# Griffin-style encoder block in split fp32: operand refills and weight sums dealt out by K tiles, and three more idle products at the start

## The chip, the core and the metric

One core of a Trainium2 chip runs the whole block in one launch. The metric is the device time of one execution in microseconds (us), the median over runs. Names of the engines in the text: PE is TensorE, DVE is VectorE, ACT is ScalarE, POOL is GpSimd, SP is SyncE, which here only issues transfers.

## The reference

A stream of 1,024 tokens, with 16 learned meta tokens ahead of it, goes through one layer of width 1,024 in float32:

```
u = rms_norm(h) * pre_w
rq, rk, rv, rg, aq, ak, av, ag, gr, ga = split(u @ w_in)
o_r = bidirectional_retention(rotary(rq), rotary(rk), rv)      # 4 heads, chunks of 128
y_r = (group_norm(o_r) * ret_nw * silu(rg)) @ w_rb
o_a = windowed_attention(rotary(aq), rotary(ak), av, sink)     # 8 heads, window +-128
y_a = (o_a * silu(ag)) @ w_ab
mix = sigmoid(gr) * y_r + sigmoid(ga) * y_a
out = h + rms_norm(mix @ w_o) * post_w                         # the meta tokens are dropped
```

The change touches the first projection (the columns of rq and rk of the first head) and the four large products at the end: the gates rg, ag, gr, ga (four times 1,024 columns of `w_in`), `w_rb`, `w_ab` and `w_o`.

## The kernel before

**Split products.** Every float32 product is made of three on PE: each operand is split into a rounded high part h (made by ACT or POOL as a copy to the type fp32r) and a low part, operand minus h (made by DVE, `dve_lo`, L92). `mm3` issues high x high (L76), low x high (L77) and high x low (L78).

**The start.** `idle` products multiply zeros by zeros (L313, 128x384) while the first inputs arrive. Then come eight rounds, one for each K tile of 128 rows of x: ACT makes the high part `xh[k]` (L333), DVE the low part `xl[k]` (L335), and `qk0_mm(k)` (L321) issues 18 products over six outputs. Between the rounds stand small serial computations (the decays of the retention).

**The middle.** Retention (four heads), then attention, with gate projections of z filled in between.

**The end: four phases z, r, a, o.** z computes the gates in 16 units, r multiplies by `w_rb`, a by `w_ab`, o by `w_out`. Each unit is a 2x2 block product in seven products instead of eight, in the order 1, 5, 6, 2, 7, 3, 4 (units go in pairs; the first pair of z has an order of its own). The left operands of a unit are sums of its weight blocks (`prepare`: weights `wrz{u}_{j}`, sums `stz{u}S`, split into `lhz{u}_{p}` by ACT, L976, and `llz{u}_{p}` by DVE, L92); they are prepared six products ahead of their use (`LEAD`). What comes out is added up by DVE in `combine` (`u2z`, `u3z`, `c1z`: L1066) and goes on to `post`. In the phase z some partial results `e{u}{p}` come back from DRAM.

**Right operands.** The seven right operands are four plain blocks and sums of the activation: B11, T1 (product 5), T2 (6), B21 (2), T3 (7), B22 (3) and T4 (4), each of four K tiles in a high and a low part. They lie in the tiles `big` and `T` and are overwritten for the next phase as soon as their last product of the old one is done. `refill(nm, src)` brings in the operands of the phase that follows `nm`; it returns which step is to be issued behind which product, counted from the first product of that next phase (negative numbers lie in `nm`): loads of staged tiles (`stage`), differences on DVE (`minus`, L1155), and `split_b` (a copy on ACT, a difference on DVE, L92). After z and after r the sums are made on the spot from the attention's and the retention's gated outputs in DRAM (for r and a); after a the sums of `w_out`, which lie ready in DRAM, are fetched (`get_pre`) and only the plain blocks are split.

**The output weights' sums.** For the phase o the sums T1, T3, T2 and T4 of `w_out` (`SUMS`) are computed during z: `pre_load(k)` fetches the four blocks of a K tile k, and `pre_split(k, behind)` makes four differences, splits each and stores eight tiles to DRAM (`wT1`, `wT3`, `wT2`, `wT4`, and the stores `preT`, L779 and L781). `run` hangs `pre_load(k)` behind product 12k + 16 and `pre_split(k)` behind product 12k + 22, counted from the first product of z.

**What sets the order.** The program text is an order of wishes: a scheduler with a simulated timeline lays out each engine's instructions from it, by priority and by when an instruction could start, and `issue_after` forces one instruction behind another. SP issues the transfers in one row, each at its turn, so a transfer that has to wait holds up the ones behind it.

Of the kernel before, what the change touches and what calls it, by code (L numbers as in the profile page):

```python
# [7 lines left out]
F32 = mybir.dt.float32  # L8
R = mybir.dt.float32r
AF = mybir.ActivationFunctionType  # L10
ALU = mybir.AluOpType
# [23 lines left out]
def cols(c):  # L35
    return (0, NM) if c == 0 else (NM + P * (c - 1), NM + P * c)
# [3 lines left out]
def block_kernel(ctx: ExitStack, tc: tile.TileContext, x0, xT, x, meta, w_in, w_rb, w_ab, w_out, post_w,  # L40
                 rope, tab, out):
    nc = tc.nc
# [12 lines left out]
    def bank(tag, name):  # L55
# [13 lines left out]
    pre_d = {n: [dram.tile([P, 4, 512], F32, tag=f"pre{n}{s}", name=f"pre{n}{s}") for s in range(2)]  # L69
             for n in ("T1", "T2", "T3", "T4")}  # L70
# [20 lines left out]
    def dve_lo(o, i, hi):  # L91
        return nc.vector.tensor_tensor(o, i, hi.bitcast(F32), ALU.subtract).ins  # L92
# [19 lines left out]
    def halves_w(u):  # L112
        hi, lo = [], []

        def split(t, act):
            h, l = (wp.tile([P, 4, 256], R, tag=f"w{x}", bufs=4, name=f"w{x}{u}_{len(hi)}") for x in "hl")
            if act:
                nc.scalar.copy(h, t)
            else:
                pool_hi(h, t)  # L120
            hi.append(h)
            lo.append(l)
            return dve_lo(l, t, h)

        return split, ((lambda k, a, b: hi[k // 4][:, k % 4, a:b]), (lambda k, a, b: lo[k // 4][:, k % 4, a:b]))
# [140 lines left out]
    with tc.tile_pool(name="setup", bufs=1, reuse_waits="tile") as st:  # L266
# [42 lines left out]

        idle = pj("idle")  # L310
        zeros = xm.rearrange("p k e -> p (k e)")
        for i in range(8):
            nc.tensor.matmul(idle[:, 0:KT * (32 + NM)], zeros[:, 0:P], zeros, start=True, stop=True)  # L313


# [38 lines left out]
        split, wv0 = halves_w(U_V)  # L354
# [5 lines left out]
        for c in range(9):  # L360
            a, b = cols(c)
# [372 lines left out]
    def last_keys():  # L734
# [4 lines left out]
    SUMS = ("T1", (0, 0), (0, 1), (0, 0)), ("T3", (0, 1), (1, 1), (0, 1)), ("T2", (1, 1), (1, 1), (0, 0)), (  # L739
        "T4", (1, 0), (1, 0), (1, 1))  # L740
# [23 lines left out]
    def pre_load(k, src):  # L764

        w[k] = {}
        for i, j in ((0, 0), (0, 1), (1, 1), (1, 0)):
            w[k][i, j] = t = stage(f"w{i}{j}{k}", 1)
            src(t, 4 * i + k, j)

    def pre_split(k, behind):

        x = w.pop(k)
        for n, o, a, b in SUMS:
            with tc.issue_after(behind):
                nc.vector.tensor_tensor(x[o], x[a], x[b], ALU.subtract)
            h, l = (stage(f"w{n}{k}{e_}", s, R) for s, e_ in enumerate("hl"))
            nc.scalar.copy(h, x[o])
            nc.sync.dma_start(pre_d[n][0][:, k], h.bitcast(F32))  # L779
            dve_lo(l, x[o], h)  # L780
            nc.sync.dma_start(pre_d[n][1][:, k], l.bitcast(F32))  # L781

    w, near = {}, []
    gates = [U_G + u for u in range(4)] + [U_AG + u for u in range(4)] + [U_GR + u for u in range(8)]
# [151 lines left out]
    def right(n, s, k):  # L936
        if n == "T4" and k == 3:
            return margins[s], lambda t: t.rearrange("p (a c) -> p a c", a=KT)
        return B[n][s][:, k], lambda t: t
    POST = {2: (0, 0), 7: (1, 1), 3: (0, 1), 4: (1, 0)}  # L940
    final = "o", 3, 4
    sub, mul, add = ALU.subtract, ALU.mult, ALU.add

    def stage(name, j=0, dt=F32):
        return (yp if j else lp).tile([P, 512], dt, tag=f"sg{int(j)}", bufs=8 if j else 7, name=name)
# [4 lines left out]
    def split_b(n, k, src):  # L950
        (h, as_), (l, _) = (right(n, s, k) for s in range(2))
        nc.scalar.copy(h, as_(src))
        dve_lo(l, as_(src), h)

    class Phase:
# [18 lines left out]
        def split(self, u, p, src):  # L974
            h, l = (lp.tile([P, 4, P], R, tag=t, bufs=LEAD, name=f"{t}{self.nm}{u}_{p}") for t in ("lh", "ll"))
            nc.scalar.copy(h, src)  # L976
            dve_lo(l, src, h)
            self.ops[u, p] = h, l
# [149 lines left out]
    def get_pre(n):  # L1128
        for s in range(2):
            m = B[n][s].shape[1]  # L1130
            nc.sync.dma_start(B[n][s].bitcast(F32), pre_d[n][s][:, 0:m])
            if m < 4:
                d, as_ = right(n, s, m)
                nc.sync.dma_start(d.bitcast(F32), as_(pre_d[n][s][:, m]))
# [8 lines left out]
    def refill(nm, src):  # L1143

        x = {}

        def load(i, j):
            def f():
                for k in range(4):
                    x[i, j, k] = t = stage(f"{nm}{i}{j}{k}", j)  # L1150
                    src(t, 4 * i + k, j)
            return f

        def minus(o, a, b):
            nc.vector.tensor_tensor(x[*o], x[*a], x[*b], sub)  # L1155

        def plain(n, i, j):
            def f():
                for k in range(4):
                    split_b(n, k, x[i, j, k])  # L1160
            return f

        def t1():
            for k in range(4):
                minus((0, 0, k), (0, 1, k), (0, 0, k))
                split_b("T1", k, x[0, 0, k])

        def t2():
            for k in range(4):
                minus((0, 0, k), (1, 1, k), (0, 0, k))  # L1170
                split_b("T2", k, x[0, 0, k])

        def t3():
            for k in range(4):
                minus((0, 1, k), (1, 1, k), (0, 1, k))

        def b21():
            for k in range(4):
                split_b("B21", k, x[1, 0, k])
                minus((0, 0, k), (1, 0, k), (0, 0, k))  # L1180

        def got(n):
            return lambda: get_pre(n)

        if nm == "a":
            return {-16: [load(0, 0)], -14: [load(1, 1)], -13: [plain("B11", 0, 0)], -11: [got("T1")],
                    -10: [load(1, 0)], -9: [got("T2")], -7: [plain("B21", 1, 0)], -5: [got("T3")],
                    -3: [plain("B22", 1, 1)], -1: [got("T4")]}
        return {-16: [load(0, 0), load(0, 1)], -14: [load(1, 1)], -13: [plain("B11", 0, 0)], -11: [t1],
                -10: [load(1, 0)], -9: [t2, t3], -7: [b21], -5: [plain("T3", 0, 1)], -3: [plain("B22", 1, 1)],  # L1190
                -1: [plain("T4", 0, 0)]}

    def run(phases):

        jobs = [(ph, u, p) for ph, _ in phases for u, p in ph.seq]
        hooks, i = {}, 0
        for ph, src in phases:
            i += len(ph.seq)
            if src:
                hooks.update({i + j: f for j, f in refill(ph.nm, src).items()})  # L1200

        for u in (0, 1):
            hooks.setdefault(len(jobs) - len(ph_o.seq) - 11 + u, []).insert(0, lambda u=u: ph_o.block(u, "A11"))
        for k in range(4):
            hooks[12 * k + 16] = [lambda k=k: pre_load(k, act_src(w_out))]
            hooks[12 * k + 22] = [lambda k=k: pre_split(k, near[0])]
        n = 0
        for i, (ph, u, p) in enumerate(jobs):
            while n < min(i + LEAD, len(jobs)):
                q, u_, p_ = jobs[n]  # L1210
                q.prepare(u_, p_)
                n += 1
            yield
            ph.product(u, p)
            for f in hooks.get(i, ()):
                f()
# [6 lines left out]
    def act_src(d):  # L1223
        def src(o, k, j):
            nc.sync.dma_start(o, d[k, :, 512 * j:512 * j + 512])
        return src
# [122 lines left out]
    def o_tail(o, a):  # L1349
# [4 lines left out]
        if a:  # L1354
            with tc.issue_after(scaled):
                for c, t, _ in parts:
# [6 lines left out]
            (3, 4)]  # L1363
    ph_o = Phase("o", seq, o_load, o_post, apart=(0, 1))
    steps = run([(Phase("z", sequence(16, (1, 3, 2, 5, 6, 7, 4)), w_loader(w_in, gates), z_post, z_fetch,
                        early=(0, 1), pre=PRE),
                  act_src(oTr_d)),
# [211 lines left out]
    i = attention()  # L1579
# [105 lines left out]
```

## Time and profile before

| what | us |
|---|---|
| median of three runs (1043.12, 1043.39, 1044.73) | 1043.39 |
| the profiled execution | 1044.06 |
| its span, first to last instruction | 1042.3 |
| PE busy | 1025.3 (98%) |
| PE's weight loads busy | 898.8 (86%) |
| DVE busy | 834.9 (80%) |
| ACT busy | 502.5 (48%) |
| POOL busy | 227.9 (22%) |

The mean clock that PE was granted is 0.998 of full speed. The page gives the busy time of each engine; the list of waits says for a line how long its engine stood idle ahead of it, and which instruction of another engine ended that (us in total, times, longest); the timeline lists instructions in order with their start, length, engine, line and operation, `out<-in`, and in brackets the idle time before them and what ended it. A row of SPq is a transfer's issue; in the list of transfers the last number is the median time from issue to landing. In a table by stages, the columns behind the busy times of the engines are the granted clock, the busy share of the 16 DMA engines, and the GB/s that they moved. Names of tiles are given without their numbers in the profile's rows: `u2z` stands for the `u2z` tile of any unit.

### The profile page before, as it was taken

The numbers are of one execution on the slowest core, as the hardware profiler recorded it, in microseconds if no ns is written. First come the engines' busy times: TensorE is split into PE (matmuls) and PEld (weight loads), VectorE is DVE, ScalarE is ACT, GpSimd is POOL, SyncE is SP. The second block draws the span as 40 slices with busy tenths as digits, with TensorE's granted clock in tenths as the row PEclk, the third lists the DMA queues.
The fourth block names the chain that finished last, engine by engine and source line by source line (L and its number), as shares of the span: only waits on it lengthen the run. The fifth ranks groups of instructions, "written<-read, shape, count | busy, mean of one in ns | idle before, by whom it ended". The sixth has DMA issues, their size and how long they took to land. (4 is left out here: it accounts for less than half of the span.)

```text
span 1042.3 us, 17315 instructions
## 1 busy us (share of the span) xinstructions
PE 1025.3 (98%) x5880; PEld 898.8 (86%) x5880; DVE 834.9 (80%) x1802; ACT 502.5 (48%) x1129; POOL 227.9 (22%) x368
## 2 busy tenths in 40 slices
PE   8999999999999999999999999999999999999997
PEld 8998999989989888988888888777888788788886
DVE  7786769758876778778769988998899899778665
ACT  5541332523423466664676554555557446334443
POOL 3345244243342433444310000000000000111032
PEclk9999999999999999999999999999999999999999
DMA  9434123243241467675558679899925746789464
GB/s 355 164 84 90 62 45 89 76 79 112 80 93 62 102 174 188 179 194 157 171 174 322 216 255 311 309 317 346 392 106 178 251 156 222 234 219 336 130 122 81
DMA packets 98841, 188.45 MB, mean 181 GB/s; under 512 B 13025, under 2 KB 37633, under 8 KB 98193
## 3 DMA queue, kind: packets, MB, share of 16 engines
q1 hardware_dynamic: 81200, 162.89, 46.4%
q0 software_dynamic: 10176, 14.73, 9.5%
q10 hardware_dynamic: 7376, 9.73, 2.7%
q8 instruction: 46, 0.75, 0.3%
q14 instruction: 43, 0.34, 0.1%
HBM read 124.32 MB, written 57.68 MB: 175 GB/s over the span
## 5 line engine op out<-in xcount | busy, mean ns | idle before, releaser
L1289 POOL DMA_DIRECT2D mx_d<-c1a x4 | 3.6, 890 | 398.1 <-DVE c1a L1280 398.1
L77 PE MATMUL bz<-big,llz 128*128 128x512 f32 x192 | 74.8, 390 | 0.3 <-DVE llz L92 0.3
L76 PE MATMUL bz<-big,lhz 128*128 128x512 f32 x192 | 74.0, 390 | 1.1 <-ACT lhz L976 1.1
L78 PE MATMUL bz<-big,lhz 128*128 128x512 f32 x192 | 74.2, 389 | 0.0
L76 PE MATMUL pv<-wh,big 128*128 128x256 f32 x256 | 72.8, 284 | 0.0
L77 PE MATMUL pv<-wh,big 128*128 128x256 f32 x256 | 72.7, 284 | 0.0
L78 PE MATMUL pv<-wl,big 128*128 128x256 f32 x256 | 72.7, 284 | 0.0
L76 PE MATMUL bz<-T,lhz 128*128 128x512 f32 x176 | 68.2, 390 | 1.4 <-DVE u2z L1066 1.3
L77 PE MATMUL bz<-T,llz 128*128 128x512 f32 x176 | 68.6, 390 | 0.9 <-DVE llz L92 0.9
L78 PE MATMUL bz<-T,lhz 128*128 128x512 f32 x176 | 68.5, 389 | 0.0
L76 PE MATMUL paq<-big,wh 128*128 128x512 f32 x128 | 51.5, 403 | 0.0
L1429 ACT ACTIVATE p<-raw,nm 128x337 f32<-128x337 f32 (+1 forms) x64 | 35.5, 556 | 33.1 <-DVE nm L1426 31.6
L77 PE MATMUL paq<-big,wl 128*128 128x512 f32 x128 | 50.3, 393 | 0.0
L78 PE MATMUL paq<-big,wh 128*128 128x512 f32 x128 | 50.2, 392 | 0.0
L1442 POOL TENSOR_SCALAR p<-p,den 128x336 f32<-128x336 f32 (+2 forms) x60 | 34.6, 624 | 66.7 <-DVE den L1433 64.1
L76 PEld LDWEIGHTS pv<-wh,big 128*128 128x128 f32 x256 | 48.4, 189 | 0.4
L77 PEld LDWEIGHTS pv<-wh,big 128*128 128x128 f32 x256 | 48.3, 189 | 0.4
L78 PEld LDWEIGHTS pv<-wl,big 128*128 128x128 f32 x256 | 48.2, 188 | 0.3
L76 PEld LDWEIGHTS bz<-big,lhz 128*128 128x128 f32 x192 | 36.0, 188 | 8.8 <-ACT lhz L976 1.5
L92 DVE TENSOR_TENSOR wl<-wr,wh 128x1024 fp32r<-128x1024 f32 x28 | 35.1, 1257 | 10.0 <-POOL wh L89 6.8
L77 PEld LDWEIGHTS bz<-big,llz 128*128 128x128 f32 x192 | 36.0, 188 | 8.1 <-DVE llz L92 0.6
L78 PEld LDWEIGHTS bz<-big,lhz 128*128 128x128 f32 x192 | 36.0, 188 | 7.5
(621 smaller groups left out, 3592.8 us busy)
## 6 DMA issues: line engine op xcount, KB each, us to landing
wrz<-in_w_in_dram SPq DMA_DIRECT2D x32, 512.0 KB, 6.1
wr<-in_w_in_dram SPq DMA_DIRECT2D x29, 512.0 KB, 4.1
we<-in_w_in_dram SPq DMA_DIRECT2D x16, 512.0 KB, 4.3
tg<-tg_d SPq DMA_DIRECT2D x32, 256.0 KB, 4.9
e<-e ACTq DMA_DIRECT2D x20, 256.0 KB, 2.6
e<-e SPq DMA_DIRECT2D x20, 256.0 KB, 4.7
xn<-in_x_dram SPq DMA_DIRECT2D x8, 512.0 KB, 9.0
oTr_d<-ost SPq DMA_DIRECT2D x16, 256.0 KB, 2.1
```

Of the source, the lines that this page charges most:

```text
L76: nc.tensor.matmul(o, ah, bh, start=first, stop=False, **kw)
L77: nc.tensor.matmul(o, al, bh, start=False, stop=False, **kw)
L78: latest[:] = [nc.tensor.matmul(o, ah, bl, start=False, stop=last, **kw).ins]
L92: return nc.vector.tensor_tensor(o, i, hi.bitcast(F32), ALU.subtract).ins
L1289: nc.gpsimd.dma_start(d, to, accum_op=ALU.add)
L1429: last["exp"] = nc.scalar.activation(pp[:, x_, w0 - o:w0 - o + 1 + wid], r[:, 0:1 + wid], AF.Exp, scale=-1.0, bias=nm_[:, x_:x_ + 1], accu ...
L1442: nc.gpsimd.tensor_scalar(v, v, den[:, x_:x_ + 1], 1.0, op0=ALU.mult, op1=ALU.mult)
```

## The change

- The start issues 11 idle products instead of 8.
- `pre_split` makes one of the four sums at a call instead of all: they hang behind the products 12k + 21 to 12k + 24, each with its own `near[0]` (DVE's last addition into a unit's result) to be issued behind.
- `refill` deals its steps out by K tiles, one or two to a product instead of four behind one product, After z and r, T2 and B21 come later than before, and T3, B22 and T4 stand behind the products 1 to 8 of the new phase itself; one tile of B21's load is issued eight products later than the others. After a, the splits keep their places but for the dealing out. The operations are the same in number and kind.
- `run` collects several steps for one product in a list.

```diff
--- before.py
+++ after.py
@@ -309,7 +309,7 @@
 
         idle = pj("idle")
         zeros = xm.rearrange("p k e -> p (k e)")
-        for i in range(8):
+        for i in range(11):
             nc.tensor.matmul(idle[:, 0:KT * (32 + NM)], zeros[:, 0:P], zeros, start=True, stop=True)
 
 
@@ -768,17 +768,19 @@
             w[k][i, j] = t = stage(f"w{i}{j}{k}", 1)
             src(t, 4 * i + k, j)
 
-    def pre_split(k, behind):
-
-        x = w.pop(k)
-        for n, o, a, b in SUMS:
-            with tc.issue_after(behind):
-                nc.vector.tensor_tensor(x[o], x[a], x[b], ALU.subtract)
-            h, l = (stage(f"w{n}{k}{e_}", s, R) for s, e_ in enumerate("hl"))
-            nc.scalar.copy(h, x[o])
-            nc.sync.dma_start(pre_d[n][0][:, k], h.bitcast(F32))
-            dve_lo(l, x[o], h)
-            nc.sync.dma_start(pre_d[n][1][:, k], l.bitcast(F32))
+    def pre_split(k, i, behind):
+
+        n, o, a, b = SUMS[i]
+        x = w[k]
+        with tc.issue_after(behind):
+            nc.vector.tensor_tensor(x[o], x[a], x[b], ALU.subtract)
+        h, l = (stage(f"w{n}{k}{e_}", s, R) for s, e_ in enumerate("hl"))
+        nc.scalar.copy(h, x[o])
+        nc.sync.dma_start(pre_d[n][0][:, k], h.bitcast(F32))
+        dve_lo(l, x[o], h)
+        nc.sync.dma_start(pre_d[n][1][:, k], l.bitcast(F32))
+        if n == "T4":
+            del w[k]
 
     w, near = {}, []
     gates = [U_G + u for u in range(4)] + [U_AG + u for u in range(4)] + [U_GR + u for u in range(8)]
@@ -1144,51 +1146,44 @@
 
         x = {}
 
-        def load(i, j):
+        def load(i, j, ks=range(4)):
             def f():
-                for k in range(4):
+                for k in ks:
                     x[i, j, k] = t = stage(f"{nm}{i}{j}{k}", j)
                     src(t, 4 * i + k, j)
             return f
 
         def minus(o, a, b):
-            nc.vector.tensor_tensor(x[*o], x[*a], x[*b], sub)
-
-        def plain(n, i, j):
-            def f():
-                for k in range(4):
-                    split_b(n, k, x[i, j, k])
-            return f
-
-        def t1():
+            return lambda k: nc.vector.tensor_tensor(x[*o, k], x[*a, k], x[*b, k], sub)
+
+        def split(n, i, j):
+            return lambda k: split_b(n, k, x[i, j, k])
+
+        def each(at, n, *fs):
             for k in range(4):
-                minus((0, 0, k), (0, 1, k), (0, 0, k))
-                split_b("T1", k, x[0, 0, k])
-
-        def t2():
-            for k in range(4):
-                minus((0, 0, k), (1, 1, k), (0, 0, k))
-                split_b("T2", k, x[0, 0, k])
-
-        def t3():
-            for k in range(4):
-                minus((0, 1, k), (1, 1, k), (0, 1, k))
-
-        def b21():
-            for k in range(4):
-                split_b("B21", k, x[1, 0, k])
-                minus((0, 0, k), (1, 0, k), (0, 0, k))
+                at.setdefault(n + k if len(fs) > 1 else n + k // 2, []).extend([lambda f=f, k=k: f(k) for f in fs])
 
         def got(n):
             return lambda: get_pre(n)
 
+        at = {-16: [load(0, 0)] + ([] if nm == "a" else [load(0, 1)]), -14: [load(1, 1)]}
+        each(at, -13, split("B11", 0, 0))
         if nm == "a":
-            return {-16: [load(0, 0)], -14: [load(1, 1)], -13: [plain("B11", 0, 0)], -11: [got("T1")],
-                    -10: [load(1, 0)], -9: [got("T2")], -7: [plain("B21", 1, 0)], -5: [got("T3")],
-                    -3: [plain("B22", 1, 1)], -1: [got("T4")]}
-        return {-16: [load(0, 0), load(0, 1)], -14: [load(1, 1)], -13: [plain("B11", 0, 0)], -11: [t1],
-                -10: [load(1, 0)], -9: [t2, t3], -7: [b21], -5: [plain("T3", 0, 1)], -3: [plain("B22", 1, 1)],
-                -1: [plain("T4", 0, 0)]}
+            at.update({-11: [got("T1")], -10: [load(1, 0)], -9: [got("T2")], -5: [got("T3")], -1: [got("T4")]})
+            each(at, -7, split("B21", 1, 0))
+            each(at, -3, split("B22", 1, 1))
+            return at
+        each(at, -11, minus((0, 0), (0, 1), (0, 0)), split("T1", 0, 0))
+        at[-10].append(load(1, 0, range(3)))
+        each(at, -7, minus((0, 0), (1, 1), (0, 0)), split("T2", 0, 0))
+        each(at, -3, split("B21", 1, 0), minus((0, 0), (1, 0), (0, 0)))
+        at[-2].append(load(1, 0, (3,)))
+        at[1] = at.pop(0)
+        each(at, 2, minus((0, 1), (1, 1), (0, 1)))
+        each(at, 3, split("T3", 0, 1))
+        each(at, 5, split("B22", 1, 1))
+        each(at, 7, split("T4", 0, 0))
+        return at
 
     def run(phases):
 
@@ -1197,13 +1192,15 @@
         for ph, src in phases:
             i += len(ph.seq)
             if src:
-                hooks.update({i + j: f for j, f in refill(ph.nm, src).items()})
+                for j, f in refill(ph.nm, src).items():
+                    hooks.setdefault(i + j, []).extend(f)
 
         for u in (0, 1):
             hooks.setdefault(len(jobs) - len(ph_o.seq) - 11 + u, []).insert(0, lambda u=u: ph_o.block(u, "A11"))
         for k in range(4):
             hooks[12 * k + 16] = [lambda k=k: pre_load(k, act_src(w_out))]
-            hooks[12 * k + 22] = [lambda k=k: pre_split(k, near[0])]
+            for i in range(4):
+                hooks[12 * k + 21 + i] = [lambda k=k, i=i: pre_split(k, i, near[0])]
         n = 0
         for i, (ph, u, p) in enumerate(jobs):
             while n < min(i + LEAD, len(jobs)):
```

## The prediction

> **What bounds the kernel now.** I read the page's busy times first, then the list of what TensorE (PE) waited for, then the timeline at the places where it waited.
>
> ```profile
> span 1042.3 us, 17315 instructions
> PE 1025.3 (98%) x5880; PEld 898.8 (86%) x5880; DVE 834.9 (80%) x1802; ACT 502.5 (48%) x1129; POOL 227.9 (22%) x368
> ```
>
> PE is busy for 1025.3 of 1042.3 us, so all of its idle time together is 17.0 us; an edit that leaves the products as they are can win more than that only by the clock, which makes a busy product shorter. The list of PE's waits shows what of it has a releaser on another engine inside the last phases:
>
> ```profile
> PE bz L76 <- DVE u2z L1066: 1.3, 1, 1.3
> PE bz L77 <- DVE llz L92: 1.2, 2, 0.9
> PE bz L76 <- ACT lhz L976: 1.1, 1, 1.1
> PE ba L77 <- DVE lla L92: 0.9, 1, 0.9
> PE br L77 <- DVE llr L92: 0.8, 2, 0.6
> ```
>
> These are bz (phase z), br and ba (the first products after a refill): 5.3 us. The rest lies at the start, where the clock is low. The timeline of the start (start us, length us, engine, line):
>
> ```profile
> 1.36 2.93 PE L313 MATMUL idle<-xm 128*128 128x384 f32 x8 [1.36 <-DVE warm L207]
> 5.53 0.77 PE L76 MATMUL pq<-big,w 128*128 128x512 f32 x1 [1.24 <-ACT big L333]
> 9.77 0.33 PEld L78 LDWEIGHTS pq<-big,w 128*128 128x128 f32 x1
> 10.53 0.19 PEld L76 LDWEIGHTS pq<-big,w 128*128 128x128 f32 x1
> 10.65 0.39 PE L76 MATMUL pq<-big,w 128*128 128x512 f32 x1
> 13.47 0.62 PE L76 MATMUL pq<-big,w 128*128 128x512 f32 x2
> 16.28 0.39 PE L76 MATMUL pq<-big,w 128*128 128x512 f32 x1
> ```
>
> The eight idle products end at 4.29, PE stands for 1.24 us, and the first round of L321 (one k over all six outputs) takes from 5.53 to 10.65, 5.12 us, where a later round takes 16.28 - 13.47 = 2.81 us. A weight load falls from 0.33 to 0.19 us between 9.77 and 10.53: that is where the clock rises, 5.0 us after unbroken work began.
>
> **The change part by part.** The profiled execution took 1044.06 us (span 1042.3 and 1.8 around it), 0.67 above the median 1043.39 of the three timed runs, which lie between 1043.12 and 1044.73. I sum against 1044.06 and give the result as the forecast: the scatter of the runs is about what an earlier or later rise of the clock would make, and the change acts on that very term.
>
> *Eleven idle products.* Three more at 2.93 / 8 = 0.37 us end at 4.29 + 1.10 = 5.39, before the first real product at 5.53, which waits for ACT: they delay nothing, and the gap shrinks from 1.24 to 0.14 us. If what counts is 5.0 us of unbroken work, it now counts from 1.36, and the clock rises at 6.36. Then 0.83 us of the first round run low, 0.83 / 5.12 = 16% of it, and the other 84% take 2.36 us: the round ends at 8.72 instead of 10.65, 1.9 us sooner. Do the inputs keep up?
>
> ```profile
> 7.49 1.16 ACT L333 ACTIVATE big<-xr,vec 128x1040 fp32r<-128x1040 f32 x1 [1.47 <-DVE w L92]
> 8.68 1.30 DVE L335 SCALAR_TENSOR_TENSOR big<-xr,vec,big 128x1040 fp32r<-128x1040 f32 x1 [0.93 <-ACT big L333]
> 9.84 2.44 ACT L333 ACTIVATE big<-xr,vec 128x1040 fp32r<-128x1040 f32 x2 [1.19 <-DMA xr<-in_xT_dram]
> 32.37 0.36 ACT L167 COPY vmeta<-pv 16x256 f32<-16x256 f32 x1 [3.24 <-PE pv L165]
> ```
>
> Round 2's high part is there at 8.65 and its low part at 9.98 (needed for the last third, at about 10.6); round 3's high part at 9.84 + 1.22 = 11.06, needed at 11.53. So 1.9 us is just about what the inputs allow, and no more. The next piece of serial work on ACT waits for PE at 32.37, so it moves up with PE. Bounds: 0 (the clock rises at 10.5 as now) to 2.0.
>
> The Trainium skill, "TensorE: Matmul & The Clock Gate", Part 1, says that the clock is decided at the ends of free-running windows of 4096 cycles, about 3.4 us, and rises after one busy window. By that the present rise at about 10.4 would come one window sooner, near 7.0, and the start would give 1.7 instead of 1.9 us; the trace's single rise cannot tell the two apart.
>
> *The refills dealt out.* Here the diff promises more than it does. I laid the instruction orders of the two built programs side by side: of the refills' differences and splits on DVE (L1155, L92 into big and T), all three phases, every one stands where it stood, but for two pieces of T4 in z's refill that move by one place. From there to the end all engines' orders are the same, with the same waits. The scheduler had already pulled these operations to where their buffers come free. So the stalls around the two refills stay:
>
> ```profile
> 763.38 0.69 DVE L1066 TENSOR_TENSOR u3z<-u3z,bz 128x512 f32<-128x512 f32 x1 [1.39 <-ACT u3z L1063]
> ```
>
> DVE's unbroken run before br starts here, released by a product through ACT, so it starts earlier when PE is earlier and the stall is neither eaten nor added to. Term: 0. It could be 1.7 at most (the br and ba rows above).
>
> *The sums of the output weights (pre_split).* These do move, for k = 1 and 2 (k = 3 keeps its order), and the stalls of phase z stand there. PE's and DVE's timelines:
>
> ```profile
> 668.39 0.39 PE L76 MATMUL bz<-big,lhz 128*128 128x512 f32 x1
> 669.85 0.50 PE L76 MATMUL bz<-big,lhz 128*128 128x512 f32 x1 [1.07 <-ACT lhz L976]
> 670.49 0.50 PE L76 MATMUL bz<-T,lhz 128*128 128x512 f32 x1
> 697.39 0.39 PE L76 MATMUL bz<-big,lhz 128*128 128x512 f32 x1
> 699.08 0.50 PE L76 MATMUL bz<-T,lhz 128*128 128x512 f32 x1 [1.31 <-DVE u2z L1066]
> 720.75 0.61 PE L76 MATMUL bz<-T,lhz 128*128 128x512 f32 x2
> 722.31 0.50 PE L77 MATMUL bz<-T,llz 128*128 128x512 f32 x1 [0.94 <-DVE llz L92]
> 677.85 0.69 DVE L1002 TENSOR_TENSOR stz8S<-wrz,wrz 128x512 f32<-128x512 f32 x1 [1.77 <-DMA wrz<-in_w_in_dram]
> 697.75 0.68 DVE L92 TENSOR_TENSOR llz<-stz9S,lhz 128x512 fp32r<-128x512 f32 x1
> 698.35 0.68 DVE L1066 TENSOR_TENSOR u2z<-e,bz 128x512 f32<-128x512 f32 x1
> 710.74 0.69 DVE L1002 TENSOR_TENSOR stz10S<-wrz,wrz 128x512 f32<-128x512 f32 x1 [3.17 <-DMA wrz<-in_w_in_dram]
> 721.57 0.68 DVE L92 TENSOR_TENSOR llz<-stz10S,lhz 128x512 fp32r<-128x512 f32 x1
> ```
>
> Where nothing waits, a product starts 0.22 us after the one before (720.75: two of them in 0.61, the second of 0.39). From 668.39 to 670.49 PE makes two such steps in 2.10 us and loses 1.66; at 697 one in 1.69, a loss of 1.47; at 721 two in 1.56 (720.75 to 722.31), a loss of 1.12: 4.2 us. Each is the end of a long run of DVE at 0.60 us an operation (697.75 to 698.35), and the runs at 677.85 and 710.74 begin when a weight load wrz lands. So what counts is how many operations stand between that load's first user and the awaited one, and when the load lands.
>
> At 697: stz8S and the awaited u2z8 are 34 places apart now, 32 in the changed order, as two operations come ahead of the load into time in which DVE idled (1.77 us): 2 x 0.60 = 1.2 us sooner. At 668 the distance from the first user of wrz6_1 is 37 in both, so that stall may stay; but PE then only waits there instead of at 697. At 721 the run is the same 18 places, and its start hangs on the landing of wrz10_1:
>
> ```profile
> 703.14 2.69 SPq L1220 DMA_DIRECT2D wrz<-in_w_in_dram x2
> wrz<-in_w_in_dram SPq DMA_DIRECT2D x1, 512.0 KB, 7.6
> 700.00:710.00 10.00, 10.00 (x46) 8.27 (x45) 7.53 (x13) 4.49 (x8) 0.00 (x0) 1.00 1.05 375
> ```
>
> The DMA engines are full there (1.05) and move 375 GB/s, 0.70 us for 256 KB. In SP's new order one 256 KB load (e113) moves behind wrz10_1: 0.7 us sooner; and what goes before it comes from a DVE run that is up to 1.2 us earlier: 0.7 to 1.9 us. PE is then ahead of DVE at 721, so this landing is what phase z gains in the end, whatever the two stalls before it do. I take 1.5, since both parts point the same way, for z. Bounds: 4.2 (all three stalls gone) to -3.8 (the last rival).
>
> After that no PE wait is left before the refill of z, and no other engine's order changes (POOL's is the same). The 64 sums and splits are the same in number and cost; SP issues the same DMAs. Sum: 1044.06 - 1.9 - 1.5 = 1040.7 us.
>
> **The rivals.**
>
> *The clock rises as before.* A gap of 0.14 us is left, and the trace shows no rise with any gap behind it. Then the start gives nothing: 1044.06 - 1.5 = 1042.6. Against it: 0.14 us is less than half of one idle product (0.37), hardly a stop.
>
> *Phase z gains nothing.* The DMA engines are full, so the order of the transfers in SP's queue only trades one for another, and PE waits at 721 as now: 1044.06 - 1.9 = 1042.2. For it: the run at 721 has its old length.
>
> *Phase z is cleared.* DVE, let loose earlier before each load, stays ahead: 1044.06 - 1.9 - 4.2 = 1038.0. Against it: DVE has almost no idle time between 646 and 735 other than its waits for wrz.
>
> *The refills do act after all,* through the times at which their loads are waited for: 1.7 us more, 1039.0. Against it: the same order and waits.
>
> *Slower.* In SP's new order the last store of k = 1's sums stands ahead of the load e73, one w_out load and the loads wrz9_0 and wrz8_1, and SP waits in order:
>
> ```profile
> 665.71 0.51 SPq L993 DMA_DIRECT2D e<-e x1
> 670.22 0.33 SPq L781 DMA_DIRECT2D preT<-wT41l x1
> ```
>
> If SP stands at that store, wrz8_1 lands late, and everything from 677.85 on is late with it. Up to 1.2 us the shorter run of DVE pays for it; it decides beyond 1.2 us for z, and beyond 3.1 us for the kernel. A hold of 5 us (about 670.22 - 665.71, by which the store now follows e73) costs 5.0 - 1.2 = 3.8: 1044.06 - 1.9 + 3.8 = 1046.0. Against it: the split wT41l that the store waits for comes three places earlier on DVE.
>
> **How the numbers follow.** About 0.2%, 2.1 us, is what a measurement of this kernel can tell from no change: below 1041.3 is faster, above 1045.5 slower. Forecast 0.55 (its own range 1039.9 to 1041.6, of which 0.08 lies above 1041.3); clock as before 0.13; z gains nothing 0.17; z cleared 0.06; refills act 0.04; slower 0.05. Faster: 0.47 + 0.06 + 0.04 = 0.57; same: 0.08 + 0.13 + 0.17 = 0.38; slower 0.05. The range 1039.0 to 1042.8 leaves out z cleared and slower (0.11) and the edges of the other cases.
>
> **What would show it.** In the changed profile: weight loads of 0.19 us from 6.4 to 7.0 us on, and round 2 starting near 8.7; the wait at 697 gone or under 0.5 us; the one at 721 still there, 1.1 us or more, at an earlier time; the br and ba waits at their old sizes. I am wrong if weight loads take 0.33 us until 10, if the 721 wait is gone (then z is cleared), or if DVE's wait for wrz at 677.85 ends later than 679.

## The result and the profile after

The changed kernel runs in 1040.84 us (median of 10 runs, 1039.93 to 1042.62), against 1043.44 us (median of 10, 1041.29 to 1044.73) for the kernel before on the same chip: a ratio of 0.9979, 95% interval 0.9969 to 0.9989. By the ratio it is faster by 2.2 us (1.1 to 3.2), and the forecast of 1040.7 is met. The steps behind it are met only in part.

The profiled execution after took 1040.10 us, span 1038.3. The two profiled executions thus lie 3.96 us apart, where the medians lie 2.60 apart: the one before was 0.6 above its median, the one after 0.7 below. Read alone, the pair of traces overstates the change by half.

The page's span and busy times after:

```profile
span 1038.3 us, 17311 instructions
PE 1023.7 (99%) x5883; PEld 898.0 (86%) x5883; DVE 835.8 (80%) x1802; ACT 502.6 (48%) x1129; POOL 228.0 (22%) x368
```

PE's idle time falls from 17.0 to 14.6 us, and its busy time by 1.6, since a product is shorter at the full clock. The list of PE's waits after (us in total, times, longest), against the five rows of before:

```profile
PE bz L76 <- DVE u2z L1068: 1.1, 1, 1.1
PE ba L77 <- DVE lla L92: 0.9, 1, 0.9
PE br L77 <- DVE llr L92: 0.8, 2, 0.6
PE bz L76 <- ACT lhz L978: 0.3, 1, 0.3
PE bz L77 <- DVE llz L92: 0.2, 1, 0.2
```

Phase z's waits (bz) fall from 3.6 to 1.6 us; those behind the two refills (br and ba) stay at 0.8 and 0.9. The start after, from PE's timeline and that of its weight loads:

```profile
1.36 3.79 PE L313 MATMUL idle<-xm 128*128 128x384 f32 x11 [1.36 <-DVE warm L207]
5.47 0.47 PE L76 MATMUL pq<-big,w 128*128 128x512 f32 x1 [0.32 <-ACT big L333]
8.84 0.47 PE L76 MATMUL pq<-big,w 128*128 128x512 f32 x1 [0.30 <-ACT big L333]
5.44 0.19 PEld L76 LDWEIGHTS pq<-big,w 128*128 128x128 f32 x1 [0.69 <-POOL w L89]
```

The first real weight load already takes 0.19 us: the clock is up (the trace's record of the granted clock has the rise at 4.92 us). The second round begins at 8.84 instead of 10.65 and now waits for ACT's high part, so the inputs set this stretch. At the end of the first head's products (the same instruction at 43.70 before and 42.08 after) 1.62 us are won, where z begins 1.21, where r begins 3.94, at the end of the span 4.0. The stretch between gave 0.4 back, z won 2.7 in this pair, and r, a and o nothing.

In z the three stalls changed places. The one at 668 is gone, the one at 721 is gone, and the one at 697 stays, now at 694.29. PE's and DVE's timelines:

```profile
694.29 0.39 PE L76 MATMUL bz<-big,lhz 128*128 128x512 f32 x1
695.81 0.50 PE L76 MATMUL bz<-T,lhz 128*128 128x512 f32 x1 [1.13 <-DVE u2z L1068]
667.78 0.68 DVE L1068 TENSOR_TENSOR u2z<-u2z,bz 128x512 f32<-128x512 f32 x1
671.00 0.69 DVE L1068 TENSOR_TENSOR u2z<-e,bz 128x512 f32<-128x512 f32 x1 [2.53 <-DMA e<-e]
```

The unbroken run of DVE that ends at PE's wait now begins at 671.00 with the arrival of e73, the load that SP's new order put behind the stores of K tile 1. DVE stood idle for 2.53 us ahead of it, and from there to u2z8 (695.07) it is 40 operations. One wait for a load has taken the place of another.

### The profile page after: what moved, and what is told of

It is laid out like the page before. It is cut to its first block, busy times and chain, and to the rows that moved or that the text cites. A ratio compares the mean times of both kernels' runs of the same rounds, so it can differ in the third digit from the quotient of the medians.

```text
span 1038.3 us, 17311 instructions
## 1 busy us (share of the span) xinstructions
PE 1023.7 (99%) x5883; PEld 898.0 (86%) x5883; DVE 835.8 (80%) x1802; ACT 502.6 (48%) x1129; POOL 228.0 (22%) x368
## 5 line engine op out<-in xcount | busy, mean ns | idle before, releaser
L92 DVE TENSOR_TENSOR wl<-wr,wh 128x1024 fp32r<-128x1024 f32 x28 | 35.1, 1258 | 10.4 <-POOL wh L89 6.7
```

## Experiments: each part alone

All times are medians, and each ratio is to the runs of the kernel before on the same chip in the same job, with its 95% interval. "Waits of bz" is the sum of the phase's rows in the list of PE's waits of one profiled execution.

| kernel | us | ratio | bz | br, ba |
|---|---|---|---|---|
| before | 1043.44 | 1 | 3.6 | 0.8, 0.9 |
| changed | 1040.84 | 0.9979 (0.9969 to 0.9989) | 1.6 | 0.8, 0.9 |
| e1: 11 idle products only | 1041.22 | 0.9981 (0.9972 to 0.9990) | 1.1 | 0.8, 0.9 |
| e2: sums only | 1041.77 | 0.9992 (0.9984 to 1.0001) | 1.5 | 0.8, 0.9 |
| e3: refills only | 1042.24 | 1.0000 (0.9991 to 1.0009) | 1.8 | 0.8, 0.9 |

**e1, the idle products.** Edit:

```diff
-        for i in range(8):
+        for i in range(11):
             nc.tensor.matmul(idle[:, 0:KT * (32 + NM)], zeros[:, 0:P], zeros, start=True, stop=True)
```

> Only the 11 idle products; sums and refills as before. My theory: PE is then at work without a gap from 1.36 us, the clock rises between 4.8 and 7 us instead of at 10.4, and the time falls by 1.2 to 1.9 us against the kernel before (the changed kernel's trace is 1.6 us ahead at 44 us and 1.2 us ahead where phase z begins). The three stalls of phase z at 668, 697 and 721 stay, 1.7, 1.5 and 1.1 us. Rival: the rise is a matter of luck and not of the idle products; then the time is within 0.4 us of before and weight loads of 0.33 us are seen until about 10 us.

1041.22 us, 0.9981: the idle products win 2.0 us by the ratio (1.0 to 2.9), 1.2 by the medians (the kernel before ran at 1042.39 there). The clock rose at 6.27 us. But z's waits are 1.1 us here, though in z DVE, ACT, POOL and SP have the order of before, which had 3.6.

**e2, the sums.** Edit: `pre_split` and its hooks as in the change, all else as before.

> Only the sums of the output weights dealt out; 8 idle products, refills as before. My theory on record: phase z gains 1.5 us. The changed kernel's trace: it gains 2.7 us, the stalls at 668 and 721 are gone and the one at 697 stays at 1.7 us. If that is the work of the sums alone, this kernel shows the same three readings, and the time falls by 1.5 to 2.7 us. Rival: the stalls went because PE came earlier by the start; then phase z keeps 4.2 us of stalls here and the time is within 0.4 us of before.

1041.77 us, 0.9992: 0.8 us, with an interval that just reaches no change. The stalls near 668 and 721 are gone and the one at 697 stays (0.8 us ahead of 696.57), as in the changed kernel: that pattern is the work of the sums alone. What it is worth is less sure. From z's first product to r's first, z takes 245.5 us after the change and 245.3 here, but in the order of before 248.2, 245.3 (e1) and 246.0 (e3). Added to the idle products (the changed kernel against e1) the sums bring 0.2 us by the ratios and 1.4 by the medians.

**e3, the refills.** Edit: `refill` and the list of hooks as in the change, all else as before.

> Only the refills dealt out; 8 idle products, sums as before. My theory: in the built program only one DVE operation and one store move by one or two places, so the time is within 0.4 us of before and the stalls behind the two refills keep their sizes, 0.4 and 0.75, 1.06 and 0.17 us. Rival: the refills do act, 0.5 to 1.7 us faster, with smaller waits of br and ba.

1042.24 us, 1.0000, with br and ba waits of the old size. Beside this, its trace holds two surprises. z's waits are 1.8 us, although its order in z is that of before with 3.6: e1, e3 and before are three executions of one order in z, with 1.1, 1.8 and 3.6 us. And the clock was up at the first real product with 8 idle products and PE idle ahead of it (weight loads of e3):

```profile
5.37 0.19 PEld L76 LDWEIGHTS pq<-big,w 128*128 128x128 f32 x1 [1.59 <-POOL w L89]
```

## Experiments: which K tile, and how far apart

**e4, only K tile 0 dealt out, and e8, all but K tile 0.** Edits to the changed kernel (e8 has `k > 0` instead):

```diff
-                hooks[12 * k + 21 + i] = [lambda k=k, i=i: pre_split(k, i, near[0])]
+                hooks.setdefault(12 * k + (21 + i if k == 0 else 22), []).append(
+                    lambda k=k, i=i: pre_split(k, i, near[0]))
```

> The changed kernel, but only the sums of K tile 0 are dealt out; those of K tiles 1 to 3 come all four behind one product (12k + 22), as before. Theory landing: the stall at 668 went because the stores of K tile 0 left SP's row sooner and the load wrz6_1 landed 3.2 us earlier; then it is gone here too, wrz6_1 lands 3 us earlier against the place of phase z, and 697 or 721 keep a stall of 1 us or more. Theory distance: what counts is the number of DVE operations between the load and the awaited one in K tile 1's stretch; then 668 keeps 1.2 us or more here. Time 1041 to 1042.5 under the first, 1042 to 1043 under the second.

> The changed kernel, but the sums of K tile 0 come all four behind product 22, as before; those of K tiles 1 to 3 are dealt out. The mirror of e4. If K tile 0's dealing is what frees SP's row for wrz6_1, the stall near 667 is back here at 0.7 us or more, and the time is 0.5 to 1.7 us above e4. If the dealing of any K tile does equally well, the time is within 0.4 us of e4 and 667 has no stall.

e4: 1039.74 us, 0.9967 (0.9955 to 0.9979), below what either theory gave: no stall near 668, and 1.6 us of bz waits, the longest 1.0 us at 698. e8: 1041.09 us, 0.9990 (0.9981 to 1.0000), and the stall is back:

```profile
669.32 0.47 PE L76 MATMUL bz<-T,lhz 128*128 128x512 f32 x1 [0.90 <-DVE u2z L1068]
```

So it is K tile 0 that pays: the intervals of e4 and e8 lie apart. Dealing it out is worth 1.5 us from e1 to e4, and 1.1 (by the ratios) or 1.5 (by the medians, each against the kernel before of its own job) from e8 to the changed kernel. Dealing out the later ones (e1 to e8, e4 to the changed kernel) brings nothing by the medians and costs 0.9 to 1.3 us by the ratios. SP's rows say how K tile 0 does it: ahead of the loads wrz7_0 and wrz6_1 stood K tile 0's last stores and K tile 1's loads. Before (the two wrz at 639.11) and after:

```profile
632.18 2.41 SPq L1225 DMA_DIRECT2D w<-in_w_out_dram  x4
634.69 0.38 SPq L781 DMA_DIRECT2D preT<-wT40l  x1
639.11 1.08 SPq L1220 DMA_DIRECT2D wrz<-in_w_in_dram  x2
```

```profile
631.16 0.32 SPq L781 DMA_DIRECT2D preT<-wT40l  x1
633.65 0.44 SPq L1217 DMA_DIRECT2D wrz<-in_w_in_dram  x1
635.83 0.46 SPq L1217 DMA_DIRECT2D wrz<-in_w_in_dram  x1
```

The store of T4's low part goes out 3.5 us sooner, the loads wrz7_0 and wrz6_1 5.5 and 4.0 us sooner, of which 1.2 is the whole kernel's lead at that point. Before, DVE's run up to the stall began with a piece of wrz7_0, by way of ACT's high part of it:

```profile
646.28 0.69 DVE L92 TENSOR_TENSOR llz<-wrz,lhz 128x512 fp32r<-128x512 f32 x1 [2.38 <-ACT lhz L976]
```

wrz7_0 had landed at 645.55, and wrz6_1, which the run's third operation needs, at 646.97. They are now 4.3 and 2.8 us less late, DVE doesn't stop there, and the stall was 1.7. Thirteen of the traces agree (all but e5, which has no sums). In the four with K tile 0 in one lump (before, e1, e3, e8) DVE stands before this operation for 2.4, 0.8, 1.1 and 0.8 us, and PE stalls near 668 by 0.5 to 1.1 us. In the nine with K tile 0 dealt out DVE waits for these two loads by 0.6 us at most, and PE doesn't stall there.

**e7 and e11, 16 products apart instead of 12.** Edit to e4, giving e7 (e11 makes the same one to the changed kernel, where all four K tiles are dealt out):

```diff
-            hooks[12 * k + 16] = [lambda k=k: pre_load(k, act_src(w_out))]
+            hooks.setdefault(16 * k + 16, []).append(lambda k=k: pre_load(k, act_src(w_out)))
...
-                hooks.setdefault(12 * k + (21 + i if k == 0 else 22), []).append(
+                hooks.setdefault(16 * k + (21 + i if k == 0 else 22), []).append(
```

> The kernel of e4 with the four K tiles of the sums 16 products apart instead of 12 (loads behind product 16k + 16, sums behind 16k + 21 and on). Theory: the stalls of z come where the DMA engines are full, up to about 720 us; spread over a longer stretch the loads land sooner, z keeps under 0.6 us of stalls, and the time is 0.5 to 1.5 us below e4. Rival: the load is only moved, and the last K tile now meets the refill: a stall of 1 us or more near 790 to 815, and the time is that of e4 or above.

> The changed kernel (all four K tiles of the sums dealt out) with the K tiles 16 products apart instead of 12. It tells whether e7 gains by the distance alone. Theory distance: phase z has under 0.6 us of stalls, and the time is that of e7, 0.996 of the kernel before. Theory dealing: what counts is that only K tile 0 is dealt out, and this one is at 0.998, like the changed kernel, with stalls of 1 us or more in z.

e7: 1038.56 us, 0.9959 (0.9946 to 0.9971); bz waits 0.3 us, all of it at z's first products, so z is cleared. e11: 1043.50 us, 1.0009 (0.9999 to 1.0020). The distance alone is not it. With the later K tiles dealt out as well, DVE falls behind later in z and at the refill. Six of e11's eleven runs were also granted less clock (0.994 to 0.997, where e7 had 0.998 or 0.999 in all five); the other five ran in 1041.3 to 1042.8, so most of the loss is there without that. Waits of e11:

```profile
PE bz L77 <- DVE llz L92: 2.2, 3, 1.0
PE br L77 <- DVE llr L92: 1.9, 2, 1.3
```

Why four pieces behind one product do better there than four behind four products isn't settled; some 50 of DVE's operations and 25 of SP's transfers stand elsewhere.

**e5, z without the sums.** Edit: the hooks of `pre_load` and `pre_split` are left out, and eight plain copies of the weights' halves into `pre_d` stand in attention, so the output is not the reference's.

> The kernel before (8 idle products) without the sums of the output weights in phase z: their loads, 32 DVE operations, 16 ACT copies and 32 stores are left out, and the eight tiles in DRAM are filled by plain copies of the weights during attention, so the output is not the reference's. It prices all that a rearrangement of the sums can bring. Theory: phase z's stalls near 668, 697 and 721 come of this load on DVE and the DMA engines; they go, and the time falls by 2 to 4 us against before. Rival: the stalls come of z's own work (stores, gates, weights); then at least half of them stay, and the time falls by less than 1 us.

1045.16 us, 1.0024 (1.0013 to 1.0035): slower. The trace points at the copies, which delay the attention where they were put, but no run moves them, and the trace is that of the fastest of the eleven runs, 2.6 us under the median. Rows of the waits of e5, the first two from attention (before has none for kTh and 0.2 us for pm):

```profile
PE ps L76 <- ACT kTh L715: 2.4, 2, 1.6
PE pt L1460 <- POOL pm L89: 1.4, 2, 1.1
PE bz L77 <- DVE llz L92: 1.3, 3, 0.9
```

The total can't price the sums. What can be read is that z still waits 1.3 us without them, so part of its waits is its own; the expected clearing did not come. z takes 245.2 us here, no less than in e1 with all the sums in it (245.3).

## Experiments: the refills, and the idle products again

**e9 and e10, the low parts of B22 and T4 held back.** In the changed kernel the br stall reads like this on DVE (the second row is three operations):

```profile
803.49 0.69 DVE L92 TENSOR_TENSOR llr<-str0S,lhr 128x512 fp32r<-128x512 f32 x1
804.70 1.89 DVE L92 TENSOR_TENSOR big<-z,big 128x512 fp32r<-128x512 f32 x3
807.70 0.68 DVE L92 TENSOR_TENSOR llr<-str1S,lhr 128x512 fp32r<-128x512 f32 x1
808.44 0.50 PE L77 MATMUL br<-big,llr 128*128 128x512 f32 x1 [0.24 <-DVE llr L92]
```

The rows big<-z are T4's last piece and pieces of B22, wanted by the products 10 to 13 of r; PE waits for llr1_5, its product 3, which stands behind them. The change names products 5 to 8 of r for these pieces, and the scheduler made them earlier all the same. Edit, to e7 (e9) and to the changed kernel (e10):

```diff
     def split_b(n, k, src, behind=None):
...
-        dve_lo(l, as_(src), h)
+        with tc.issue_after(lows[behind]) if behind else ExitStack():
+            dve_lo(l, as_(src), h)
...
-        each(at, 5, split("B22", 1, 1))
-        each(at, 7, split("T4", 0, 0))
+        each(at, 5, split("B22", 1, 1, (1, 6)))
+        each(at, 7, split("T4", 0, 0, (1, 6)))
```

Here `lows[u, p]` is the low part of the left operand of unit u's product p, noted in `Phase.split`.

> The kernel of e7, and the low parts of B22 and T4 of the two refills (8 DVE operations each) are forced behind the low part of the new phase's product (1, 6). That is what dealing them into the next phase says but did not do, since the scheduler pulled them up. Theory: the stalls of br and ba are DVE doing operations that PE needs only at products 10 to 13, ahead of those it needs at product 3 and 4; 8 operations at 0.60 us are 4.8 us, more than the stalls, which go: 1.5 to 2.4 us below e7, about 1036.5. Rival: DVE or SP is then late with B22 or T4 (its staging tiles are held longer and the loads behind them wait); a stall of 1 us or more comes up later in r or a, and the time is that of e7 or above.

> The changed kernel with the same forced order of B22 and T4 as e9. Theory: 1.5 to 2.4 us below the changed kernel, which ran at 0.998 of the kernel before: 0.9955 to 0.9965 of it. Rival: as in e9, no gain: 0.998 or above.

e9: 1036.27 us, 0.9945 (0.9932 to 0.9957). e10: 1037.35 us, 0.9959 (0.9947 to 0.9972). Neither list of waits has a br or ba row any more. DVE of e9:

```profile
807.28 0.68 DVE L92 TENSOR_TENSOR llr<-str0S,lhr 128x512 fp32r<-128x512 f32 x1
808.60 0.68 DVE L92 TENSOR_TENSOR llr<-str1S,lhr 128x512 fp32r<-128x512 f32 x1
809.20 2.49 DVE L92 TENSOR_TENSOR big<-z,big 128x512 fp32r<-128x512 f32 x4
811.61 1.89 DVE L92 TENSOR_TENSOR T<-z,T 128x512 fp32r<-128x512 f32 x3
```

The same operations come behind the awaited ones, and nothing is late later on. e10 against the changed kernel is 2.1 us by the ratios, e9 against e7 1.5 by the ratios and 2.3 by the medians: the br and ba waits and what is lost beside them. e9 is the fastest kernel of this study, 5.7 us below the kernel before.

**e6, the refills' differences on POOL.** Edit to e4: `nc.gpsimd.tensor_tensor` for `nc.vector.tensor_tensor` in `minus`.

> The kernel of e4 with the 32 differences of the two refills (16 each) on POOL instead of DVE. Theory: the stalls behind the refills (br 0.4 and 0.77 us, ba 1.07 and 0.17) come of the length of DVE's unbroken run, which dealing out cannot shorten; 16 operations fewer at 0.60 us are 9.6 us, so the stalls go, and the time is 1.5 to 2.4 us below e4. Rival: the differences are slower on POOL (over 0.7 us each) and slow DVE beside them, or the stalls hang on when the old operands come free; then the stalls stay and the time is that of e4 or above.

1056.79 us, 1.0136 (1.0118 to 1.0154): the rival, and far worse than it said. One such group in the profile of e6, and the same 20 us in e4 and e6 (busy times and counts of PE, PEld, DVE, ACT, POOL, then clock, DMA share, GB/s):

```profile
L1157 POOL TENSOR_TENSOR z<-z,z 128x512 f32<-128x512 f32 x16 | 26.8, 1698 | 246.7 <-DVE big L92 238.4 <-DMA z<-oTr_d 7.1 <-DVE T L92 1.3
760.00:780.00 20.00, 20.00 (x90) 16.55 (x89) 19.35 (x20) 10.96 (x21) 13.05 (x8) 1.00 0.19 67
793.00:797.00 4.00, 0.36 (x1) 0.36 (x2) 4.00 (x7) 2.04 (x4) 0.78 (x1) 0.54 0.37 102
```

```profile
760.00:780.00 20.00, 20.00 (x90) 16.57 (x89) 19.96 (x34) 13.42 (x26) 0.00 (x0) 1.00 0.26 88
```

A difference takes 1.70 us on POOL, and DVE beside it gets 20 operations done where e4 has 34: 0.97 instead of 0.59 us each. The 9.6 us taken off DVE are more than eaten. PE then waits 6.5 us in one piece (790.1 to 796.6), and in the middle of it, at 793.3, the granted clock falls to half.

**e12, e9 with 8 idle products.** Edit: the range of e1, back to 8.

> The kernel of e9 with 8 idle products instead of 11, so that nothing but the start differs from e9 and no stall of the later phases blurs it. The clock records so far: with 8 idle products the clock rose at 10.4, 9.6, 8.9 and once at 4.3 us; with 11 in nine runs between 4.8 and 7.6; the place where the first head's products end lies at 43.0 to 43.7 us after a late rise and 41.8 to 42.5 after an early one. Theory draw: 8 idle products leave it to the phase of the clock's window, so the cost over many runs is about 1.1 us: 1037.1 to 1037.6, and the runs scatter wider than those of e9 (1035.3 to 1036.4). Theory on record (5 us of unbroken work, always late): 1.9 us, 1038.0 or above.

1036.75 us (1035.75 to 1039.03), 0.9953 (0.9936 to 0.9971), against 0.9945 for e9: 0.5 us by the medians, 0.8 by the ratios, 1.2 by the means of the runs. The clock rose late, at 9.46 us, and yet the profiled execution is only 0.2 us longer than e9's. The runs scatter wider, but those of the kernel before did so as well on this chip (1038.82 to 1044.23, against 1040.48 to 1044.45 beside e9). Taken together, the intervals of the two ratios allow a difference of some -1.4 to 3.1 us, so this pair alone rules out neither 1.9 us nor none.

## Why the prediction was right, and where its steps were not

- **The sum.** 1044.06 - 1.9 - 1.5 = 1040.7 against 1040.84. Both errors that it holds cancel: the base, the profiled execution, was 0.6 us above its median, and the two terms together (3.4) are above what the change gives (2.2, 1.1 to 3.2). That the number came within 0.2 us is in good part luck.
- **Eleven idle products, 1.9 us: right in sign, by a wrong step, and probably too large.** e1 gives 2.0 (1.0 to 2.9) by the ratio and 1.2 by the medians, e12 against e9 0.5 to 1.2, which is not clear of noise; the first head's products end at 41.8 to 42.5 us in the nine executions with 11 and at 42.3 to 43.7 in the five with 8, 0.9 us apart on the mean. The step that failed is "5.0 us of unbroken work": with 11 idle products the rise came 3.6 us after PE's start (3.5 to 6.2 in the nine traces), and in e3 3.0 us after it, with 8 and a gap behind them. Round 2 began at 8.84, near the forecast 8.72, but the clock had risen 1.4 us sooner than assumed and ACT's high part set the start. The rival "the clock rises as before" is refuted by all nine clock records. The Trainium skill's rule of free-running windows ("TensorE: Matmul & The Clock Gate", Part 1), which the prediction put at 1.7 us, is the one that the traces bear out (below). The trace before could have told the two apart: its full clock lasts 301 windows of 3.413 us, and the window that ends at 6.98, one before the rise, is the one with the gap in it. The rule makes the rise before a draw and not a fixed time, so the term is smaller on average than in the one trace that I had.
- **The refills, 0: right**, for the reason given. e3 is at 1.0000, and its br and ba waits are the old ones. e9 and e10 show what the dealing out would have brought had the order followed it, 1.5 to 2.3 us.
- **The sums, 1.5 us: places wrong, sign and size not settled.** e2 alone gives 0.8 us (-0.1 to 1.7), and beside the idle products they give 0.2 to 1.4, so 1.5 lies near the upper end. The prediction kept the stall at 668 because the number of operations behind wrz6_1 was the same; it went, because this load was issued 4.0 us sooner and wrz7_0 5.5. I had looked at the landing only for wrz10_1, and left K tile 0 aside, which e4 and e8 show to be the one that counts. It saw 697 go because two operations came ahead of wrz8_1; it stayed, because the wait for e73 took that place. It saw 721 stay, and that is gone: wrz10_1 was issued 3.7 us sooner and landed 5.1 us sooner (705.57 against 710.71), where PE is 2.7 us ahead (720.75 before); the prediction had 0.7 to 1.9. Issue and PE after:

```profile
699.44 1.56 SPq L1217 DMA_DIRECT2D wrz<-in_w_in_dram  x2
718.05 0.62 PE L76 MATMUL bz<-T,lhz 128*128 128x512 f32 x2
```

  By its own test ("wrong if the 721 wait is gone") this part of the reasoning failed.
- **The slower rival** (SP standing at K tile 1's last store) did not come: wT41l is done at 661.85 and its store goes out at 663.84, with no hold. What did come is its milder form: the load e73 behind that store, and DVE waiting for it.
- **A stall in one trace is not a constant.** before, e1 and e3 share the order of z and wait 3.6, 1.8 and 1.1 us in it. The bound "4.2 us, all three stalls" was that of an unlucky execution. What makes the difference between executions isn't settled.
- **Smaller misreadings, which move no term.** Of PE's 17.0 us of idle time, the 11.7 that aren't bz, br or ba waits do not lie at the start: 2.6 do, and 7.0 lie behind PE's last product, which ends at 1035.3. ACT's order changes too, since the copies of the sums' high parts move with them. And where it counts 64 sums and splits, there are 32 on DVE, 16 differences and 16 splits, beside 16 copies on ACT.

## What to carry to other kernels

Before a stall in one profiled execution is priced, look where that execution lies among the runs, and for a second trace of the same order. A hook or a place in the program's text doesn't move an operation under a scheduler: compare the built orders, and where the order matters, force it with a dependence, as e9 did with sixteen operations. What a new order of a shared transfer queue does is told by the issue time of each load that starts a run of the busy engine, not by the count of operations behind it alone.

## What the runs showed of the hardware

- **The clock moves in steps of 3.413 us.** In every trace the stretch at full clock is a whole number of these: 1030.825 us are 302 of them after the change, 1027.412 are 301 before, 1023.998 are 300 in e9, and in e6 the clock falls for 3.413 and for 6.827 us. The Trainium skill ("TensorE: Matmul & The Clock Gate", Part 1) gives 4096 cycles, 3413 ns, for the window; the traces agree. With 8 idle products it rose at 10.4, 9.6, 8.9, 9.5 and 4.3 us, with 11 in nine executions between 4.8 and 7.6.
- **Not all of a window need be busy.** In e3 the window that ended at 4.32 held idle products from 1.36 to 4.29, 86% of it, and the clock rose; so it did in e7 (2.95 us, 86%). In e8 (rise at 7.57) the window that ended at 4.15 held 2.79 us, 82%, and it did not rise; nor did it in e9 (81%) and e11 (78%), nor in the windows with the gap behind 8 idle products (64 to 67% in before, e2, e5 and e12).
- **It falls by the same windows.** A stop of 1.6 us (e5, in attention) leaves it up; one of 6.5 us (e6) brings it down for 6.8 us, and two of 2.6 and 2.5 us in phase r for 3.4 us each. In all fourteen traces it fell behind each window in which PE was busy for 43% or less (e6's last) and stayed up behind each with 51% or more (e8's last but one).
- **POOL's and DVE's operations on 128x512 fp32 are not independent**: 1.70 us on POOL, and DVE's own grow from 0.59 to 0.97 us beside them.
